# Two-layer hybrid decoder trunk on one core: the down product called block by block on a new pace, and sums formed beforehand given to other blocks

## The chip, the cores and the metric

The kernel runs on one core of a Trainium2 chip. The metric is device time in microseconds (us) of that core, from the start of the execution to its end; smaller is better. A profiled execution is one such run with the hardware profiler on; its span runs from the program's first to its last instruction.

Engine names: PE is the matrix engine (PEld its weight loads), DVE the vector engine, ACT the scalar engine, POOL the GpSimd engine, SP the engine that here only issues DMAs. Each engine works through a list of its own in order, and waits on semaphores for what others make.

## The reference

Two layers; each is a gated mixer and a SwiGLU feed-forward block over 256 tokens of width 2048, in float32. Only the feed-forward half is touched by the change; the mixer half is cut here.

```python
def reference(x, ...):
    for l in range(DEPTH):                       # DEPTH = 2
        ...
        x = x + mixed @ w_out[l]
        h2 = rms_norm(x, norm2_g[l])             # (1, 256, 2048)
        x = x + (jax.nn.silu(h2 @ w_gate[l]) * (h2 @ w_up[l])) @ w_down[l]
    return x                                     # w_gate, w_up: (2048, 5632); w_down: (5632, 2048)
```

## The kernel before, in words

**Exact products from split operands.** Each weight tile of 128 x 1024 float32 (512 KB) is loaded into a `raw` buffer (7 of them, filled by SP in the order of line 89) and split in two by `split2`: ACT casts it to `wh` (line 100, 5 buffers), DVE subtracts to get the rest, `wl` (line 101, 4 buffers). `mm3` then makes each product with three matmuls of 128 x 512 (lines 130, 131, 132). A tile of the plain product (`unit`) feeds 12 matmuls, a tile of the feed-forward product (`s_unit`) feeds 6, so one costs PE twice what the other does, and ACT and DVE the same.

**Gate and up together by a seven-product scheme.** The 5632 hidden columns are cut into NFF = 11 blocks of 512 (numbered 0 to 10). For each, `seven` forms gate and up at once with a Strassen-like scheme: 28 tiles instead of 32. In the first half of a block there are four pieces i = 0 to 3 of five tiles each; some of the tiles are sums of weights: `s1` (line 639), `t2` (line 640) and `b12` (line 644), three adds of 128 x 1024 on DVE for each piece. After `t2` has been used, another weight is added onto it by an accumulating DMA that POOL issues (line 647), and it is kept in one of four buffers. In the second half the block takes eight more tiles, four fresh loads `b21` and the four kept ones. Then come the small steps that end the block: four sums on PSUM banks, silu and multiply (lines 657 to 670), and the transposes `act_T` (PE line 194, ACT line 582, DVE line 583) that make the two `aT` pairs that the down product reads. A block yields 30 times, once for each tile and twice more; `k` counts these steps.

**Sums formed beforehand.** For six pairs (block, piece), listed in `PRE`, `presum` forms the three sums early in the layer, during the mixer, and writes them to DRAM (`sums`). Such a piece loads `s1`, `t2` and `b12` and DVE makes no adds for it. In the kernel before, these are pieces 2 and 3 of block 0 and all four of block 1. Where such a piece has an even i, the last weight isn't added onto `t2` by DMA: DVE adds it (line 679) from `b21` after that tile has been split.

**The down product beside it.** `down(blocks)` multiplies a group of finished blocks by `w_down`: for each of four column blocks n it takes two PSUM banks (`dacc`), copies the residual `xres` into them (ACT, line 702, one copy for each of two token tiles), runs two `unit`s for each block, and copies the banks back to `xres` (ACT, line 721). The same two banks serve every n, so the next n starts when the copies out and in are done. Call this a change of bank: four ACT copies. `std_stream` picks the blocks: before, it takes a group when at least `CHUNK[0]` = 2 blocks are finished and not yet taken (or all that are left), at most `CHUNK[1]` = 3. The main loop at the end of a layer (lines 752 to 762) walks through the steps of `seven` and, after each step, asks for down units until their number has caught up with a straight line in k. Before, that line starts at k = 60 and rises by 76 units in 270 steps; when no group is ready, the loop goes on with `seven` and catches up later. The last 12 units (`TAIL`) follow after the last block. The mixer's tail has taken the first 8 steps of `seven` already (`LEAD`).

The framework below then orders each engine's list by its own priorities, so lists differ a little from the order of the code.

Of the kernel before, what the change touches and what calls it, by code (L numbers as in the profile page):

```python
# [16 lines left out]
ALU = mybir.AluOpType  # L17
# [22 lines left out]
NI = 3584 // NB  # L40
NFF = DFF // NB
ND = D // NB
PRE = ((0, 2), (0, 3), (1, 0), (1, 1), (1, 2), (1, 3))
PRE_AT = ((20, 29, 38, 48, 57, 66), (4, 16, 28, 40, 54, 66))
LEAD = 8
STEPS = 30
CHUNK = (2, 3)
ACT_TILES = 8
TAIL = 12
WARM = 12  # L50
# [14 lines left out]
def trunk(ctx, tc, x, xt, w_in, w_out, w_gate, w_up, w_down, sgu_w, sgu_g, consts,  # L65
          band, out):
    nc = tc.nc
# [17 lines left out]
    def raw_load(src, parts=1):  # L85
        raw = wp.tile([P, 2, NB], F32, tag="raw", name="raw", bufs=7)
        n = 2 // parts
        for i in range(parts):
            last_load[0] = nc.sync.dma_start(
                raw[:, i * n : (i + 1) * n, :], src[:, i * n : (i + 1) * n, :]  # L90
            )
        return raw

    def split2(raw):
        wh = wp.tile([P, 2, NB], F32R, tag="wh", name="wh", bufs=5)
        wl = wp.tile([P, 2, NB], F32R, tag="wl", name="wl", bufs=4)
        step = 2 if clock[0] > 1 else 1
        for j in range(0, 2, step):
            src = raw[:, j : j + step, :]
            nc.scalar.copy(wh[:, j : j + step, :], src)  # L100
            nc.vector.tensor_tensor(  # L101
                wl[:, j : j + step, :], src, f(wh[:, j : j + step, :]), ALU.subtract
            )
        return wh, wl
# [5 lines left out]
    def later(delay, fn):  # L110
        pending.append((clock[0] + delay, next(serial), fn))
# [17 lines left out]
    def mm3(acc, ah, al, wh, wl, first, last, again=False):  # L129
        nc.tensor.matmul(acc, ah, wh, start=first, stop=False, skip_group_check=again)  # L130
        nc.tensor.matmul(acc, ah, wl, start=False, stop=False, skip_group_check=again)  # L131
        nc.tensor.matmul(acc, al, wh, start=False, stop=last, skip_group_check=again)  # L132
# [113 lines left out]
    for lay in range(L):  # L246
# [241 lines left out]
        sums = {}  # L488

        def presum(b, i, early, lay=lay, sums=sums):  # L490
            keep = dp.tile([3, P, 2, NB], F32, tag=f"sum{lay}_{b}_{i}", name="sums")
            t = []
            for w, q in ((w_gate, 0), (w_up, 0), (w_up, 1)):
                if early:
                    x = tp.tile([P, 2, NB], F32, tag="aT", name="pre")
                else:
                    x = ap.tile([P, 2, NB], F32, tag="spt", name="pre", bufs=4)
                with tc.issue_after(last_load[0].ins):
                    nc.sync.dma_start(x, w[lay, b, i, q])
                t.append(x)  # L500

            def add(k):
                nc.vector.tensor_tensor(t[k], t[k], t[(k + 1) % 3], ALU.add)
                nc.gpsimd.dma_start(keep[k], t[k])

            for k in range(3):
                later(2 + k, lambda k=k: add(k))
            sums[b, i] = keep

        for at, (b, i) in zip(PRE_AT[lay], PRE):  # L510
            later(at, lambda at=at, b=b, i=i: presum(b, i, at < 48))
# [90 lines left out]
        def seven(b, lay=lay, pairs2=pairs2, ext2=ext2, act_later=act_later, sums=sums, norm2=norm2):  # L602
            bank = [pa.tile([P, NB], F32, tag="acc", name=f"m{i}") for i in range(5)]

            def s_unit(raw, m, i, op, first, last, bank=bank):
                wh, wl = split2(raw)
                for j in range(2):
                    ah, al = (op(2 * i + j, h) for h in range(2))
                    mm3(
                        bank[m], ah, al, wh[:, j, :], wl[:, j, :], first and j == 0,  # L610
                        last and j == 1, m in (0, 2),
                    )
                tick(0.5)

            def a_op(k, t):
                return lambda p, h: pairs2[p][:, h, k, t * P : (t + 1) * P]

            def e_op(n):
                return lambda p, h: ext2[p][:, h, n, :]

            kept = []
            for i in range(4):
                pre = sums.get((b, i))
                b11 = raw_load(w_gate[lay, b, i, 0])
                t2 = ap.tile([P, 2, NB], F32, tag="spt", name="t2", bufs=4)
                if pre is not None:
                    s1 = raw_load(pre[0])
                    nc.sync.dma_start(t2, pre[2])
                    b22 = raw_load(w_up[lay, b, i, 1])
                    b12 = raw_load(pre[1])  # L630
                else:
                    s1 = b11
                    b12 = raw_load(w_up[lay, b, i, 0])
                    b22 = raw_load(w_up[lay, b, i, 1])
                first, last = i == 0, i == 3
                s_unit(b11, 0, i, a_op(0, 0), first, last)
                yield
                if pre is None:
                    nc.vector.tensor_tensor(s1, b11, b12, ALU.add)  # L639
                    nc.vector.tensor_tensor(t2, s1, b22, ALU.add)  # L640
                s_unit(s1, 1, i, e_op(1), first, last)
                yield
                if pre is None:
                    nc.vector.tensor_tensor(b12, b12, b22, ALU.add)  # L644
                s_unit(t2, 3, i, e_op(2), first, last)
                if pre is None or i % 2:
                    nc.gpsimd.dma_start(t2, w_gate[lay, b, i, 1], accum_op=ALU.add)  # L647
                yield
                s_unit(b22, 4, i, e_op(3), first, last)
                yield  # L650
                s_unit(b12, 2, i, e_op(0), first, last)
                yield
                kept.append(t2)
            m0, c12, c21, c22 = (
                zp.tile([P, NB], F32, tag="z", name=v) for v in ("m0", "c12", "c21", "c22")
            )
            nc.scalar.copy(m0, bank[0])
            nc.vector.tensor_tensor(m0, bank[3], m0, ALU.add)
            yield

            def add(out, x, y):
                nc.vector.tensor_tensor(out, x, y, ALU.add)

            def gated(t, psum, sg, c):
                nc.scalar.activation(sg, psum, AF.Silu, scale=norm2["r"][t])
                nc.vector.scalar_tensor_tensor(sg, c, norm2["n"][t], sg, ALU.mult, ALU.mult)

            steps = {
                0: lambda: add(c21, bank[2], m0),
                1: lambda: (nc.scalar.copy(bank[2], c21), add(c12, bank[1], m0)),  # L670
                2: lambda: (add(c22, bank[1], c21), add(c12, bank[4], c12)),
                5: lambda: gated(0, bank[0], m0, c12),
            }
            for i in range(8):
                if i < 4:
                    b21 = raw_load(w_gate[lay, b, i, 1])
                    s_unit(b21, 0, i, a_op(1, 0), False, i == 3)
                    if (b, i) in sums and i % 2 == 0:
                        nc.vector.tensor_tensor(kept[i], kept[i], b21, ALU.add)
                else:  # L680
                    s_unit(kept[i - 4], 2, i - 4, a_op(1, 1), False, i == 7)
                yield
                steps.get(i, lambda: None)()
            later(1, lambda: gated(1, bank[2], c21, c22))
            act_later(b, [m0, c21])
            yield
# [7 lines left out]
        left = [NFF]  # L694
# [32 lines left out]
        def std_stream(down=down, pairs_f=pairs_f, left=left):  # L727
            downed = set()
            while left[0]:
                full = [b for b in sorted(pairs_f) if len(pairs_f[b]) == 2 and b not in downed]  # L730
                if len(full) >= CHUNK[0] or left[0] == len(full):
                    blocks = full[: CHUNK[1]]
                    downed.update(blocks)
                    yield from down(blocks)
                else:
                    yield False
# [3 lines left out]
        k = 0  # L740
# [9 lines left out]
        norm2["n"] = [nr[:, t : t + 1] for t in range(NTOK)]  # L750

        other = std_stream()
        done = 0
        for _ in steps:
            k += 1
            ahead = (k - CHUNK[0] * STEPS) * (8 * NFF - TAIL)
            while done * (NFF - CHUNK[0]) * STEPS < ahead and next(other, False):
                done += 1
        seven_done[0] = True
        for went in other:  # L760
# [92 lines left out]
```

## Time and profile before

| what | value |
|---|---|
| three timed runs | 1984.83, 1986.64, 1988.50 us (median 1986.64) |
| profiled execution, own time | 1985.98 us |
| its span | 1984.3 us |
| DVE busy, whole span | 1722.3 us (87%) |
| ACT busy, whole span | 1327.5 us (67%) |
| blocks 1 to 10 of layer 0 (first to last m0 add, line 658) | 319.3 to 937.5 us |
| the same in layer 1 | 1307.2 to 1925.2 us |
| bytes read from HBM | 455.17 MB, 240 GB/s over the span with the writes |

How to read it: the feed-forward stretch of a layer runs from about 260 us to 985 us of the span, and again from about 1250 us to the end. The add that forms m0 at the end of a block's first 20 tiles (line 658) stands once in each block, so its eleven starts in a layer cut the stretch into ten equal pieces of work. A row of the windows view gives, for one stretch of time, the busy time of PE, PEld, DVE, ACT and POOL with their instruction counts, the granted PE clock, the busy share of the DMA engines and GB/s.

### The profile page before, as it was taken

How to read it: one execution, taken by the hardware profiler on the slowest of the kernel's cores; microseconds unless marked ns; L12 is line 12 of the kernel's file. 1: busy time of each engine (PE TensorE's matmuls, PEld its weight loads, DVE VectorE, ACT ScalarE, POOL GpSimd, SP SyncE). 2: the span in 40 equal slices, each digit the busy share in tenths (PEclk: the TensorE clock that was granted, in tenths of full speed). 3: DMA queues.
4: the chain of work that ended last, by engine and by line, in shares of the span. 5: the costliest groups of instructions: out<-in, count | busy, mean ns of one | idle time of the engine just before them, and what ended most of it. 6: DMA issues, size and time to landing. Idle time of an engine off the chain costs nothing.

```text
span 1984.3 us, 25315 instructions
## 1 busy us (share of the span) xinstructions
PE 1937.9 (98%) x8788; PEld 1566.9 (79%) x8788; DVE 1722.3 (87%) x1816; ACT 1327.5 (67%) x1759; POOL 144.4 (7%) x162
## 2 busy tenths in 40 slices
PE   9999999999999999999999999999999999999999
PEld 7788887788787887878887888877887878878787
DVE  6767789999999999998766767899999999999994
ACT  7576568666666766766856755586766767757675
POOL 1211000000000000000012110000000000000000
PEclk9999999999999999999999999999999999999999
DMA  9858678778676876778787576787777677867783
GB/s 375 311 193 291 232 226 282 235 244 274 201 233 224 255 226 220 226 215 255 270 273 259 188 248 217 236 282 234 236 255 218 229 232 244 257 201 224 225 254 133
DMA packets 133072, 477.81 MB, mean 241 GB/s; under 512 B 14800, under 2 KB 15440, under 8 KB 132944
## 3 DMA queue, kind: packets, MB, share of 16 engines
q1 hardware_dynamic: 113904, 406.98, 56.7%
q0 software_dynamic: 19040, 69.21, 16.5%
q8 instruction: 69, 1.13, 0.2%
q14 instruction: 59, 0.48, 0.1%
HBM read 455.17 MB, written 20.97 MB: 240 GB/s over the span
## 4 chain that ended last, share of the span: by engine, by line
PE 82%; DVE 8%; issue 5%; ACT 3%; DMA 2%; POOL 1%; SPq 0%; DVEq 0%; ACTq 0%; POOLq 0%
PE m L131 12%; PE m L130 12%; PE m L132 12%; PE dacc L130 7%; PE dacc L131 7%; PE dacc L132 7%; PE acc L131 7%; PE acc L132 7%; PE acc L130 7%; DVE wl L101 4%; ACT wh L100 2%; DMA raw<-in_w_down_dram 1%; DVE raw L644 1%; PE ps_v L367 1%; PE ps_f L194 1%
## 5 line engine op out<-in xcount | busy, mean ns | idle before, releaser
L100 ACT CAST wh<-raw 128x1024 fp32r<-128x1024 f32 (+1 forms) x794 | 812.8, 1049 | 432.9 <-DVE raw L639 147.4
L101 DVE TENSOR_TENSOR wl<-raw,wh 128x1024 fp32r<-128x1024 f32 (+1 forms) x794 | 945.4, 1217 | 130.1 <-PE acc L131 53.3
L130 PE MATMUL m<-wh,ext 128*128 128x512 f32 x704 | 279.7, 399 | 15.9 <-ACT wh L100 15.7
L130 PE MATMUL dacc<-wh,aT 128*128 128x512 f32 x736 | 287.5, 394 | 2.1 <-ACT dacc L702 1.7
L132 PE MATMUL dacc<-wh,aT 128*128 128x512 f32 x736 | 286.8, 390 | 0.0
L131 PE MATMUL dacc<-wl,aT 128*128 128x512 f32 x736 | 286.6, 389 | 0.0
L131 PE MATMUL m<-wl,ext 128*128 128x512 f32 x704 | 279.4, 397 | 5.7 <-DVE wl L101 5.7
L132 PE MATMUL m<-wh,ext 128*128 128x512 f32 x704 | 275.3, 392 | 0.0
L131 PE MATMUL m<-wl,hT 128*128 128x512 f32 x528 | 208.1, 394 | 7.6 <-DVE wl L101 7.4
L101 DVE TENSOR_TENSOR wl<-t,wh 128x1024 fp32r<-128x1024 f32 x176 | 211.5, 1218 | 3.1 <-ACT wh L100 1.9
L100 ACT CAST wh<-t 128x1024 fp32r<-128x1024 f32 x176 | 183.3, 1050 | 37.2 <-DVE t L640 16.4
L132 PE MATMUL m<-wh,hT 128*128 128x512 f32 x528 | 206.8, 392 | 0.1
L130 PE MATMUL m<-wh,hT 128*128 128x512 f32 x528 | 205.3, 393 | 1.4 <-ACT m L670 0.8
L130 PE MATMUL acc<-wh,hT 128*128 128x512 f32 x448 | 179.4, 403 | 0.4 <-ACT wh L100 0.4
L131 PE MATMUL acc<-wl,hT 128*128 128x512 f32 x448 | 176.0, 393 | 1.6 <-DVE wl L101 1.5
L132 PE MATMUL acc<-wh,hT 128*128 128x512 f32 x448 | 175.8, 393 | 0.0
L130 PEld LDWEIGHTS m<-wh,ext 128*128 128x128 f32 x704 | 133.1, 189 | 49.8 <-ACT wh L100 23.4
L647 POOL DMA_DIRECT2D t<-in_w_gate_dram x82 | 70.2, 856 | 1351.0 <-DVE wl L101 1220.8
L130 PEld LDWEIGHTS dacc<-wh,aT 128*128 128x128 f32 x736 | 137.8, 188 | 36.6 <-ACT dacc L702 4.4
L131 PEld LDWEIGHTS m<-wl,ext 128*128 128x128 f32 x704 | 133.0, 189 | 40.4 <-DVE wl L101 13.9
L132 PEld LDWEIGHTS dacc<-wh,aT 128*128 128x128 f32 x736 | 138.1, 188 | 29.1
L131 PEld LDWEIGHTS dacc<-wl,aT 128*128 128x128 f32 x736 | 138.2, 188 | 28.5 <-DVE wl L101 0.3
(132 smaller groups left out, 2450.2 us busy)
## 6 DMA issues: line engine op xcount, KB each, us to landing
raw<-in_w_gate_dram SPq DMA_DIRECT2D x176, 512.0 KB, 5.9
raw<-in_w_down_dram SPq DMA_DIRECT2D x176, 512.0 KB, 4.8
raw<-in_w_up_dram SPq DMA_DIRECT2D x164, 512.0 KB, 5.6
raw<-in_w_in_dram SPq DMA_DIRECT2D x108, 512.0 KB, 5.1
t<-in_w_gate_dram POOLq DMA_DIRECT2D x82, 512.0 KB, 6.0
raw<-in_w_out_dram SPq DMA_DIRECT2D x64, 512.0 KB, 4.5
sums<-pre POOLq DMA_DIRECT2D x36, 512.0 KB, 5.4
pre<-in_w_up_dram SPq DMA_DIRECT2D x24, 512.0 KB, 6.3
```

The source lines that it names most:

```text
L100: nc.scalar.copy(wh[:, j : j + step, :], src)
L101: nc.vector.tensor_tensor(wl[:, j : j + step, :], src, f(wh[:, j : j + step, :]), ALU.subtract)
L130: nc.tensor.matmul(acc, ah, wh, start=first, stop=False, skip_group_check=again)
L131: nc.tensor.matmul(acc, ah, wl, start=False, stop=False, skip_group_check=again)
L132: nc.tensor.matmul(acc, al, wh, start=False, stop=last, skip_group_check=again)
L194: nc.tensor.transpose(ps[:, j, t * P : (t + 1) * P], blocks[t][:, j * P : (j + 1) * P], ident)
L367: nc.tensor.matmul(pv[:, r, i], pt[:, (r * n + i) * (t + 1) + b, :], zkv[b][:, cols], start=b == 0, stop=b == t,)
L644: nc.vector.tensor_tensor(b12, b12, b22, ALU.add)
L647: nc.gpsimd.dma_start(t2, w_gate[lay, b, i, 1], accum_op=ALU.add)
```

## The change

Three edits, all in the feed-forward half.

1. **PRE**: pieces 1, 2 and 3 of block 1 lose their sums formed beforehand, and piece 0 of blocks 3, 5 and 7 get them. The number stays six a layer, and `presum` runs at the same places.
2. **The last weight on t2** is always added by the accumulating DMA; the DVE add of line 679 is gone.
3. **The down product's groups and pace**: a group is taken as soon as one block is finished (at most `MOST` = 3), and the straight line starts at k = `START` = 36 and rises by 76 units in 294 steps.

```diff
-PRE = ((0, 2), (0, 3), (1, 0), (1, 1), (1, 2), (1, 3))
+PRE = ((0, 2), (0, 3), (1, 0), (3, 0), (5, 0), (7, 0))
-CHUNK = (2, 3)
+START = 36
+MOST = 3
...
-                if pre is None or i % 2:
-                    nc.gpsimd.dma_start(t2, w_gate[lay, b, i, 1], accum_op=ALU.add)
+                nc.gpsimd.dma_start(t2, w_gate[lay, b, i, 1], accum_op=ALU.add)
...
-                    b21 = raw_load(w_gate[lay, b, i, 1])
-                    s_unit(b21, 0, i, a_op(1, 0), False, i == 3)
-                    if (b, i) in sums and i % 2 == 0:
-                        nc.vector.tensor_tensor(kept[i], kept[i], b21, ALU.add)
+                    s_unit(raw_load(w_gate[lay, b, i, 1]), 0, i, a_op(1, 0), False, i == 3)
...
-                if len(full) >= CHUNK[0] or left[0] == len(full):
-                    blocks = full[: CHUNK[1]]
+                if full:
+                    blocks = full[:MOST]
...
-            ahead = (k - CHUNK[0] * STEPS) * (8 * NFF - TAIL)
-            while done * (NFF - CHUNK[0]) * STEPS < ahead and next(other, False):
+            while done * (NFF * STEPS - START) < (k - START) * (8 * NFF - TAIL) and next(other, False):
```

**Where the loads of w_down stand on SP.** The next rows are SP's list at the start of block 6 of layer 0 in the kernel before; `raw<-in_w_down` is a tile of the down product, `raw<-in_w_gate` and `raw<-in_w_up` are tiles of `seven`, and a number behind x counts equal rows in a run.

```order
L89 DMA raw<-in_w_up_dram 128x1024 x2
L89 DMA raw<-in_w_down_dram 128x1024 x2
L89 DMA raw<-in_w_gate_dram 128x1024 x5
L89 DMA raw<-in_w_up_dram 128x1024 x2
L89 DMA raw<-in_w_gate_dram 128x1024
L89 DMA raw<-in_w_up_dram 128x1024 x2
L89 DMA raw<-in_w_down_dram 128x1024 x5
L89 DMA raw<-in_w_gate_dram 128x1024
```

The same place in SP's list of the changed kernel (line 90 is line 89 of before):

```order
L90 DMA raw<-in_w_up_dram 128x1024 x2
L90 DMA raw<-in_w_down_dram 128x1024
L90 DMA raw<-in_w_gate_dram 128x1024
L90 DMA raw<-in_w_down_dram 128x1024
L90 DMA raw<-in_w_gate_dram 128x1024 x3
L90 DMA raw<-in_w_down_dram 128x1024 x2
L90 DMA raw<-in_w_gate_dram 128x1024
L90 DMA raw<-in_w_up_dram 128x1024 x2
L90 DMA raw<-in_w_down_dram 128x1024
```

Before, ten tiles of `seven` stand between two tiles of the down product, and then five of those in a row; now there are one to three between single ones or pairs.

**How far apart the changes of bank stand on ACT.** ACT's list of before, from the end of one change of bank to the start of the next, around the end of block 2 (`dacc` are the two banks, `CAST wh` the casts that every tile needs):

```order
L702 COPY dacc_3917<-xres 128x512
L100 CAST wh<-raw 128x1024
L665 ACTIVATE c_3779<-m_3394,ir_2740 128x512
L100 CAST wh<-raw 128x1024 x2
L100 CAST wh<-t_3945 128x1024
L100 CAST wh<-raw 128x1024 x4
L582 CAST aT<-ps_f 128x512 x2
L100 CAST wh<-raw 128x1024
L100 CAST wh<-t_4042 128x1024
L100 CAST wh<-raw 128x1024 x5
L721 COPY xres<-dacc_3916 128x512
```

And in the changed kernel, in block 3 (lines 699, 718 and 101 are 702, 721 and 100 of before):

```order
L699 COPY dacc_4221<-xres 128x512
L699 COPY dacc_4222<-xres 128x512
L101 CAST wh<-raw 128x1024 x6
L101 CAST wh<-t_4265 128x1024
L101 CAST wh<-raw 128x1024 x3
L718 COPY xres<-dacc_4221 128x512
L718 COPY xres<-dacc_4222 128x512
L699 COPY dacc_4361<-xres 128x512
L699 COPY dacc_4362<-xres 128x512
```

Between two changes of bank stood 15 casts, now 10.

**What DVE does in piece 0 of block 3.** Before, from the last kept tile of block 2 on (lines 639, 640 and 644 are the three adds of a piece):

```order
L101 TENSOR_TENSOR wl<-t_3700,wh 128x1024
L101 TENSOR_TENSOR wl<-raw,wh 128x1024 x2
L639 TENSOR_TENSOR raw<-raw 128x1024
L640 TENSOR_TENSOR t_3945<-raw 128x1024
L666 SCALAR_TENSOR_TENSOR c_3779<-c_3780,nr,c_3779 128x512
L101 TENSOR_TENSOR wl<-raw,wh 128x1024 x2
L644 TENSOR_TENSOR raw<-raw 128x1024
L101 TENSOR_TENSOR wl<-t_3945,wh 128x1024
```

The same place in the changed kernel (line 102 is line 101 of before):

```order
L102 TENSOR_TENSOR wl<-t_3832,wh 128x1024
L102 TENSOR_TENSOR wl<-raw,wh 128x1024 x3
L102 TENSOR_TENSOR wl<-t_4059,wh 128x1024
L666 SCALAR_TENSOR_TENSOR c_3911<-c_3912,nr,c_3911 128x512
L102 TENSOR_TENSOR wl<-raw,wh 128x1024 x3
L584 TENSOR_TENSOR aT<-ps_f,aT 128x512
```

The three adds are gone from this piece, and only splits are left.

## The prediction

> **What bounds the kernel now.** I read the page's first part, then windows of 50 us, then windows cut at the blocks, then the waits of DVE and ACT within them.
>
> ```profile
> span 1984.3 us, 25315 instructions
> PE 1937.9 (98%) x8788; PEld 1566.9 (79%) x8788; DVE 1722.3 (87%) x1816; ACT 1327.5 (67%) x1759; POOL 144.4 (7%) x162
> 800.00:850.00 50.00, 50.00 (x226) 41.28 (x225) 47.83 (x47) 35.15 (x43) 2.56 (x3) 1.00 0.70 218
> 850.00:900.00 50.00, 47.01 (x196) 36.11 (x194) 47.15 (x46) 34.01 (x39) 2.55 (x3) 0.97 0.71 231
> ```
>
> PE's 98% looks like a kernel with nothing left, but the two windows below it differ: 226 matmuls in one, 196 in the other, with PE busy 50.00 and 47.01. The fuller window gives PE's pace, 50 / 226 = 0.221 us a matmul; at that pace the second had 30 x 0.221 = 6.6 us free. Counts of instructions, not busy time, show PE's slack here. The Trainium skill ("Perfetto Trace Analysis", section Identifying the Most-Contended Engine) says so as a rule and asks for the busy share of weight loads instead. By it the 79% of PEld would leave 21%, some 417 us, open; but the full window loads weights for only 41.28 of 50 us, 83%, so the trace leaves about 4 points (roughly 80 us), and I go by the trace.
>
> Now the same by blocks, layer 0, from one m0 add to the next (columns: length, then PE, PEld, DVE, ACT, POOL busy, clock, DMA share, GB/s):
>
> ```profile
> L658 DVE TENSOR_TENSOR m<-m,m x11: 680/682/691, 319.3 to 937.5; 128x512 f32<-128x512 f32 x11
> 319.30:359.70 40.40, 39.34 (x174) 31.29 (x173) 38.95 (x39) 33.98 (x37) 1.69 (x2) 1.00 0.93 318
> 359.70:420.70 61.00, 56.93 (x242) 45.20 (x242) 58.56 (x57) 38.21 (x43) 3.40 (x4) 0.97 0.70 217
> 420.70:484.30 63.60, 63.05 (x281) 51.41 (x280) 62.06 (x60) 44.40 (x52) 3.41 (x4) 1.00 0.75 240
> 484.30:548.40 64.10, 61.62 (x272) 49.66 (x271) 60.83 (x58) 43.40 (x50) 3.42 (x4) 1.00 0.72 230
> 548.40:611.80 63.40, 63.40 (x283) 51.73 (x282) 61.21 (x58) 43.55 (x52) 3.42 (x4) 1.00 0.74 239
> 611.80:677.30 65.50, 63.27 (x279) 51.09 (x278) 62.12 (x60) 44.34 (x52) 3.40 (x4) 1.00 0.73 227
> 677.30:739.50 62.20, 62.20 (x278) 51.09 (x278) 60.89 (x58) 43.16 (x52) 3.41 (x4) 1.00 0.75 242
> 739.50:805.50 66.00, 63.68 (x275) 51.19 (x274) 61.13 (x59) 44.21 (x53) 3.44 (x4) 0.97 0.74 225
> 805.50:868.00 62.50, 62.13 (x276) 50.59 (x275) 60.92 (x57) 43.24 (x51) 3.40 (x4) 1.00 0.73 234
> 868.00:937.50 69.50, 66.82 (x284) 52.91 (x284) 63.29 (x61) 45.95 (x54) 3.40 (x4) 0.98 0.72 222
> ```
>
> DVE is busy about 61 us in each full block whatever the block's length: the ten rows add up to 590.0 us of 618.2. PE needs 0.221 x 276 = 61.0 us of its own. **Two engines are level, DVE a little ahead**, with buffers of four `wl` tiles between them, so whatever makes DVE idle lengthens the block. Good blocks take 62.2 to 63.6 us; every second one takes 64.1, 65.5, 66.0 and 69.5. What makes these longer:
>
> ```profile
> DVE aT L583 <- ACT aT L582: 9.8, 6, 2.4
> DVE wl L101 <- ACT wh L100: 4.0, 9, 0.7
> DVE wl L101 <- PE dacc L131: 3.5, 3, 2.5
> DVE wl L101 <- ACT dacc L702: 0.9, 1, 0.9
> ACT wh L100 <- DMA raw<-in_w_down_dram: 16.6, 7, 4.2
> ```
>
> (waits in 319.3 to 937.5: total us, times, longest). One such place, in DVE's and ACT's rows of the timeline:
>
> ```profile
> 508.43 4.62 DVE L101 TENSOR_TENSOR wl<-raw,wh 128x1024 fp32r<-128x1024 f32 x4
> 515.36 0.69 DVE L583 TENSOR_TENSOR aT<-ps_f,aT 128x512 fp32r<-128x512 f32 x1 [2.32 <-ACT aT L582]
> 513.80 1.05 ACT L100 CAST wh<-raw 128x1024 fp32r<-128x1024 f32 x1 [3.69 <-DMA raw<-in_w_down_dram]
> 507.94 5.76 DMA raw<-in_w_down_dram
> ```
>
> The last row is the chain of waits itself. A pair of blocks is used up before the next pair is finished, so `seven` runs alone (DVE sets the pace), and then the down product catches up in a run of loads. The first of them lands 5.76 us after its issue, ACT stands 3.69 us at its cast, and behind it in ACT's list stands the cast of `aT` for which DVE idles 2.32 us. In the run itself PE is the slow one, and DVE waits for it (`PE dacc`). Layer 0 has four such starts.
>
> **The change, part by part**, for one layer and for the stretch from block 0's m0 add to block 10's:
>
> ```profile
> L679 DVE TENSOR_TENSOR t<-t,raw x6: 1212/1217/1226, 316.4 to 1352.1; 128x1024 f32<-128x1024 f32 x6
> L640 DVE TENSOR_TENSOR t<-raw 128x1024 f32<-128x1024 f32 x36 | 44.0, 1222 | 0.9
> L101 DVE TENSOR_TENSOR wl<-raw,wh 128x1024 fp32r<-128x1024 f32 x274 | 324.1, 1218 | 11.9 <-PE dacc L131 3.5 <-ACT wh L100 3.0 <-issue 2.8
> L702 ACT COPY dacc<-xres 128x512 f32<-128x512 f32 x36 | 20.9, 593 | 0.4
> L721 ACT COPY xres<-dacc 128x512 f32<-128x512 f32 x36 | 20.6, 583 | 11.9 <-PE dacc L132 11.9
> SPq L628 <- DVE wl L101: 2.1, 3, 0.7
> t<-in_w_gate_dram POOLq DMA_DIRECT2D x82, 512.0 KB, 6.0
> ```
>
> *Adds removed.* Three of line 679 a layer at 1.22 us on an engine that is the bound: **-3.7 us** (bounds -3.7 and 0, if PE then ends last). In their place POOL issues three more accumulating DMAs, each landed in about 6.0 us and first read nine tiles later or more; behind them in POOL's list stand only others of their kind. Nothing. (One of the three adds stands just ahead of the stretch, at 316.4.)
>
> *Runs gone.* In the new order one down unit follows every two to four tiles of `seven`; the line asks for 8 units in 8 x 294 / 76 = 31 steps, and a block is finished every 30, so no group runs out. The four starts' waits go: 9.8 less two short ones of 0.2 is 9.4 us, and 3.5 us on PE's banks: **-13 us**. Bounds: 0, if the late load only moves to another cast, and -16, with the 2.8 us that DVE's splits waited for no cause that the profile names. What is late next is PE itself.
>
> *Changes of bank.* Before, the groups are (0,1), (2,3), (4,5), (6,7), (8,9) and (10): 6 x 4 = 24 changes. Now 11 x 4 = 44, so 20 more, each with 2 x 0.583 + 2 x 0.593 = 2.35 us on ACT: 47 us a layer. ACT was busy 43 to 46 us of a full block and has room for 4.7 more, but its list is in order: behind the copy that waits for PE's last matmul stand the casts that DVE and then PE need. The 36 copies out in this stretch are 18 changes; DVE's waits for `wh` and for the copy in (4.0 + 0.9 us) make 0.27 us each. 20 x 0.27 = **+5.4 us**. Bounds: 0 (the waits are elsewhere) and 20 x 0.9 = +18, at the longest single wait. I stay at the mean, since the banks now change ten casts apart, never within a run. For PE, ten casts leave several tiles of work between a bank's last matmul and its next first.
>
> *Sums given to other blocks.* Six pieces as before, three adds each, so DVE's sum is unchanged. In block 1, which ran without down units, they served fully: 40.40 us long, DVE 38.95, PE 39.34. A summed piece beside 1.33 down units (five of 30 steps, eight units) costs DVE 6.33 x 1.22 = 7.7 us and PE (30 + 16) x 0.221 = 10.2 us, so DVE would idle 2.5 us unless it works ahead; four `wl` buffers hold 4.9 us of splits. For blocks 3, 5 and 7 that is 0 to +7.4 us; two thirds carried over leave **+2.5 us**. Block 1 now gets down units early, which is what keeps it level: about 4 of them. The load of `t2` stands in SP's list and has waited at most 0.7 us for its buffer, with the loads behind it; DMA was 0.93 busy in the summed block 1 without delaying PE there, so I cost this at nothing.
>
> Sum for a layer: -3.7 - 13 + 5.4 + 2.5 = -8.8 us. Block 0 before its m0 add, the mixer and the tail (both kernels end with 4 units of earlier blocks and 8 of block 10) stay. Two layers: **-17.6 us**. Against the profiled execution's own time, 1985.98 (span 1984.3 and 1.7 around it), that is 1968.4; the median of the runs lies 0.7 higher, so I say 1969.
>
> *The clock.* The granted clock fell in three blocks of layer 0, and in none of their twins in layer 1:
>
> ```profile
> 1348.00:1407.50 59.50, 55.21 (x241) 43.79 (x241) 58.63 (x57) 38.05 (x43) 3.43 (x4) 1.00 0.69 217
> 1726.50:1793.00 66.50, 62.43 (x275) 49.88 (x274) 61.12 (x58) 44.10 (x52) 3.41 (x4) 1.00 0.73 222
> 1855.60:1925.20 69.60, 65.68 (x284) 51.69 (x283) 63.25 (x61) 45.81 (x54) 3.42 (x4) 1.00 0.70 221
> ```
>
> Lengths with a dip 61.0, 66.0 and 69.5; without, 59.5, 66.5 and 69.6. The dips cost +1.5 - 0.5 - 0.1 = 0.9 us in all, so even if they go I count nothing. The Trainium skill ("TensorE: Matmul & The Clock Gate", Part 1) puts a closed gate at half speed for a window of about 3.4 us; by it three windows would cost an estimated 5 us, and the sum would be near -23. The rows of layer 1 speak against that.
>
> **The rivals.**
>
> *All waits go.* Each block becomes like the best (62.2), the changes of bank hide behind PE, and the summed pieces carry over in full: -3.7 - 16 = -19.7 us a layer, 1986 - 39 = 1947. For it: the good blocks idle DVE by only 1.3 us. Against: two engines this level rarely stay so.
>
> *Slower by ACT's list.* The mechanism is the change of bank. The terms without it sum to -14.2 us, so 20 changes break even at 0.71 us each; DVE's single waits of this kind reached 0.7 and 0.9 us. At 0.95 us each a layer gains 20 x 0.95 - 14.2 = +4.8 us, 1996. For it: ACT's copies out waited 11.9 us in 36, for PE. Against: the mean of 0.27, and that the longest of those waits are in runs, where the copy follows its matmuls at once.
>
> *Nothing gained.* PE takes over: each catch-up went at PE's pace, and a block's 0.221 x 276 = 61.0 us stays. If the adds and half of the starts' waits are gained and the banks and summed pieces take 10 us, a layer changes by -3.7 - 6.5 + 10 = -0.2 us: 1986.
>
> *The change doesn't do what it says*, a block not being finished in time: the list orders show even spacing, so I give this nothing of its own.
>
> **How the numbers follow.** The forecast, 1955 to 1981: 0.58. All waits go, 1943 to 1955: 0.18. Nothing gained, 1981 to 1991: 0.16. Slower, above 1991: 0.08. The range, 1948 to 1988, leaves out 0.06 below, 0.05 of the case of nothing gained and the 0.08 of slower, 0.19 in all. About 0.2%, 4 us, is what a measurement of this kernel can tell from no change; so faster (below 1982.7) has 0.58 + 0.18 + 0.03 = 0.79, within 0.2% 0.13, slower 0.08.
>
> **What would show it.** Right: no block of 2 to 10 over 64 us; DVE's waits for `aT` under 3 us a layer and ACT's waits for `in_w_down` loads under 5; 176 copies into the banks in the whole run (before 96); 88 accumulating DMAs. Wrong: DVE idle more than 28 us a layer, with waits for `wh` or the bank copies above 10 us (the ACT rival), or blocks 3, 5 and 7 no shorter than blocks 2, 4 and 6 (summed pieces wasted).

## The result

| kernel | median | lowest to highest | ratio to before, 95% interval |
|---|---|---|---|
| before | 1987.01 us (4 runs) | 1984.83 to 1988.50 | 1 |
| changed | 1956.76 us (4 runs) | 1956.19 to 1958.38 | 0.985 (0.9833 to 0.9867) |

The changed kernel is 30 us faster, 1.5%. Its profiled execution took 1958.38 us with a span of 1956.2. The page's first part, of the changed kernel:

```profile
span 1956.2 us, 25423 instructions
PE 1932.7 (99%) x8788; PEld 1565.3 (80%) x8788; DVE 1714.9 (88%) x1810; ACT 1402.3 (72%) x1919; POOL 148.9 (8%) x168
```

PE has the same 8788 matmuls. DVE has six instructions less, ACT 160 more and is 75 us busier. Next the blocks of layer 0 in the changed kernel, from one m0 add to the next (columns as before: length, then busy time and count of PE, PEld, DVE, ACT, POOL, then clock, DMA share, GB/s):

```profile
319.20:371.60 52.40, 50.79 (x216) 38.97 (x215) 51.55 (x51) 38.05 (x45) 3.39 (x4) 1.00 0.76 236
371.60:434.00 62.40, 61.74 (x273) 49.90 (x272) 60.88 (x59) 47.76 (x59) 3.41 (x4) 1.00 0.74 236
434.00:494.70 60.70, 60.70 (x272) 49.78 (x271) 57.69 (x56) 47.54 (x59) 3.41 (x4) 1.00 0.81 260
494.70:555.60 60.90, 60.61 (x267) 48.62 (x266) 59.77 (x58) 45.79 (x58) 3.44 (x4) 1.00 0.72 239
555.60:616.10 60.50, 59.94 (x268) 49.14 (x267) 57.59 (x56) 46.77 (x58) 3.41 (x4) 1.00 0.80 254
616.10:678.40 62.30, 61.92 (x276) 50.40 (x275) 61.10 (x59) 46.36 (x59) 3.41 (x4) 1.00 0.74 238
678.40:737.70 59.30, 59.30 (x266) 48.81 (x265) 56.52 (x54) 45.66 (x58) 3.43 (x4) 1.00 0.80 262
737.70:800.20 62.50, 61.90 (x272) 49.63 (x272) 61.11 (x59) 46.63 (x59) 3.43 (x4) 1.00 0.72 235
800.20:862.30 62.10, 61.34 (x271) 49.56 (x270) 60.98 (x59) 46.61 (x56) 3.41 (x4) 1.00 0.73 232
862.30:924.60 62.30, 61.86 (x273) 49.86 (x273) 60.81 (x58) 47.59 (x59) 3.41 (x4) 1.00 0.74 236
```

The long blocks of 64 to 69.5 us are gone, and no block is over 62.5. The ten pieces hold the same tiles of `seven`, but not equal work, as the matmul counts show: block 1 now has 216 instead of 174, because down units run beside it, and block 10 has 273 instead of 284. So the whole stretch is the fair comparison; 76 loads of `w_down` stand in it in both kernels. DVE's busy time is nearly what it was, 588.0 us in ten blocks (before 590.0); its idle time fell from 28.2 to 17.4. The stretch takes 605.4 us instead of 618.2, 12.8 less, and in layer 1 (1294.3 to 1899.2) 604.9 instead of 618.0, 13.1 less. With 2.1 us at the end of layer 1 that is the whole difference of the spans. DVE's waits in the stretch (total us, times, longest), changed kernel:

```profile
DVE wl L102 <- ACT wh L101: 10.9, 25, 1.0
DVE wl L102 <- issue: 1.2, 2, 0.8
DVE wl L102 <- PE dacc L132: 1.0, 1, 1.0
DVE wl L102 <- PE m L132: 0.4, 1, 0.4
DVE c L662 <- PE m L133: 0.2, 1, 0.2
DVE aT L584 <- ACT aT L583: 0.5, 1, 0.5
```

The waits for `aT` and for PE's banks went from 9.8 and 3.5 us to 0.5 and 1.0. The waits for ACT's casts grew from 4.0 (and 0.9 for a copy into the banks) to 10.9. Both signs were forecast; the balance came out larger.

Of the signs that the prediction named for being right, all came: the longest of blocks 2 to 10 takes 62.5 us, DVE waits 0.5 us for `aT`, and ACT's waits for loads of `w_down` (the same stretch), the accumulating DMAs and the copies into the banks (152 and 24, together 176) read:

```profile
ACT wh L101 <- DMA raw<-in_w_down_dram: 0.3, 1, 0.3
t<-in_w_gate_dram POOLq DMA_DIRECT2D x88, 512.0 KB, 5.8
L699 ACT COPY dacc<-xres x152: 581/592/616, 307.2 to 1902.2; 128x512 f32<-128x512 f32 x152
L699 ACT COPY acc<-xres x24: 581/591/605, 926.1 to 1941.3; 128x512 f32<-128x512 f32 x24
```

One half of a sign of being wrong came too: the waits for `wh` are above 10 us. The other half, DVE idle more than 28 us, did not.

### The profile page after: what moved, and what is told of

Same layout as the page of the kernel before. It is cut to its first block, busy times and chain, and to the rows that moved or that the text cites. A ratio compares the mean times of both kernels' runs of the same rounds, so it can differ in the third digit from the quotient of the medians.

```text
span 1956.2 us, 25423 instructions
## 1 busy us (share of the span) xinstructions
PE 1932.7 (99%) x8788; PEld 1565.3 (80%) x8788; DVE 1714.9 (88%) x1810; ACT 1402.3 (72%) x1919; POOL 148.9 (8%) x168
## 4 chain that ended last, share of the span: by engine, by line
PE 76%; DVE 12%; issue 7%; ACT 4%; DMA 1%; POOL 1%; SPq 0%; DVEq 0%; ACTq 0%; POOLq 0%
PE m L132 11%; PE m L131 11%; PE m L133 10%; DVE wl L102 7%; PE acc L132 7%; PE dacc L131 7%; PE acc L133 7%; PE acc L131 7%; PE dacc L132 7%; PE dacc L133 7%; ACT wh L101 2%; DVE raw L640 2%; DVE t L641 1%; PE ps_f L195 1%; PE ps_v L368 1%
## 5 line engine op out<-in xcount | busy, mean ns | idle before, releaser
L647 POOL DMA_DIRECT2D t<-in_w_gate_dram x88 | 75.4, 857 | 1340.5 <-DVE wl L102 1165.3
```

## The experiments

Each ratio is against runs of the kernel before on the same chip; all carry a 95% interval. Theory W says that the catch-up runs cost and that the even spacing removes them; the rivals are named in the expectations.

| label | what differs | median, us | ratio (interval) |
|---|---|---|---|
| pace_alone | before, with new groups and line | 1960.63 | 0.9874 (0.9859 to 0.9889) |
| spread_alone | before, with the new PRE | 2012.12 | 1.0133 (1.0118 to 1.0149) |
| adds_alone | before, without the DVE adds | 1989.00 | 1.002 (1.0011 to 1.003) |
| old_sums | changed, with the old PRE | 1957.76 | 0.9864 (0.9848 to 0.988) |
| single_old_line | before, with single blocks | 1959.15 | 0.9869 (0.9855 to 0.9882) |
| runs_of_four | changed, down units in runs | 2014.39 | 1.0144 (1.0128 to 1.0159) |
| double_banks | changed, twice the changes of bank | 1986.65 | 1.0007 (0.9998 to 1.0016) |
| no_sums | changed, no sums beforehand | 1982.77 | 0.9988 (0.9979 to 0.9997) |
| before_raw8 | before, eight raw buffers | 1980.07 | 0.9974 (0.9964 to 0.9984) |
| sums_early | changed, sums in blocks 0 and 1 only, other pieces | 1955.47 | 0.9849 (0.9836 to 0.9863) |
| sums_early_raw8 | the same with eight raw buffers | 1957.98 | 0.9865 (0.985 to 0.9881) |
| pairs_slow_line | before, with a slower line | 1965.71 | 0.9898 (0.9883 to 0.9914) |

**The three parts, one at a time.** `pace_alone` is the changed kernel with these lines put back:

```diff
-PRE = ((0, 2), (0, 3), (1, 0), (3, 0), (5, 0), (7, 0))
+PRE = ((0, 2), (0, 3), (1, 0), (1, 1), (1, 2), (1, 3))
...
+                if pre is None or i % 2:
+                    nc.gpsimd.dma_start(t2, w_gate[lay, b, i, 1], accum_op=ALU.add)
...
+                    if (b, i) in sums and i % 2 == 0:
+                        nc.vector.tensor_tensor(kept[i], kept[i], b21, ALU.add)
```

> The new groups and pace alone; the sums stay with block 1 and the DVE add of line 679 stays. Theory W (the even pace removes the waits at the starts of the catch-up runs, some 16 us a layer, and pays about 6 us a layer in changes of bank; the sums only keep blocks level): blocks 2 to 10 take about 62.4 us each as the changed kernel's blocks without sums do, block 1 about 50, so 612 us a layer for the stretch against 605 in the changed kernel: about 1969 us. Rival S (the spread sums carry the gain, because they relieve DVE where down units run beside the block, and the pace alone only trades waits for changes of bank): 1980 us or more.

Measured 1960.63, 24.4 us under the kernel before on its chip. Rival S falls; W's number was 8 us too high. Its interval and that of the changed kernel overlap only at their ends.

`spread_alone` is the kernel before with only this:

```diff
-PRE = ((0, 2), (0, 3), (1, 0), (1, 1), (1, 2), (1, 3))
+PRE = ((0, 2), (0, 3), (1, 0), (3, 0), (5, 0), (7, 0))
```

> The sums spread to blocks 1, 3, 5 and 7, with the old groups of two blocks, the old pace and the DVE add. Theory W: the four catch-up starts a layer stay, and block 1, without down units beside it, loses three of its summed pieces where DVE alone sets the pace: 1987 us, between 1982 and 1994. Rival S: 1972 us or less.

Measured 2012.12, 27 us slower than before. W's number was too low as well, though its reason shows. Block 1 of layer 0 in `spread_alone`:

```profile
320.50:369.50 49.00, 42.28 (x171) 31.43 (x170) 48.33 (x48) 32.94 (x37) 2.53 (x3) 0.97 0.67 209
```

Without down units beside it and with three summed pieces fewer, the block takes 49.0 us instead of 40.4; DVE is busy all but 0.7 us, and PE has only 171 matmuls to do. That is 8.6 of the 14.0 us by which the stretch of layer 0 is longer. The blocks that got the sums return nothing in all: blocks 3, 5 and 7 took 62.9, 63.8 and 67.2 us (before 63.6, 63.4 and 62.2). In block 7 another effect of this edit shows. The DVE add of line 679 stays here for summed pieces with an even i, and the new list has five such pieces a layer instead of three, so there are 10 of these adds in the run instead of 6. One of them makes DVE wait in block 7 for its load:

```profile
DVE t L679 <- DMA raw<-in_w_gate_dram: 2.8, 1, 2.8
```

The changed kernel has none of these adds, so the 27 us are not the price of moving the sums alone.

`adds_alone` is the kernel before with only this:

```diff
-                if pre is None or i % 2:
-                    nc.gpsimd.dma_start(t2, w_gate[lay, b, i, 1], accum_op=ALU.add)
+                nc.gpsimd.dma_start(t2, w_gate[lay, b, i, 1], accum_op=ALU.add)
...
-                    if (b, i) in sums and i % 2 == 0:
-                        nc.vector.tensor_tensor(kept[i], kept[i], b21, ALU.add)
```

> Only the three DVE adds a layer of line 679 are replaced by accumulating DMAs. Theory W: 3 x 1.22 us a layer at most where DVE is the bound, so 1980 to 1985 us. Rival P (PE ends last in those blocks, so the adds were hidden): 1987 us.

Measured 1989.00, 0.2% slower than before, which neither W nor P gave. ACT's waits in block 1 of layer 0, `adds_alone`, and then the block's window:

```profile
ACT wh L100 <- DMA raw<-sums: 3.5, 3, 2.1
ACT wh L100 <- PE m L132: 2.8, 5, 1.5
ACT wh L100 <- DMA raw<-in_w_up_dram: 1.8, 1, 1.8
ACT wh L100 <- DMA raw<-in_w_gate_dram: 1.4, 1, 1.4
```

```profile
319.40:363.00 43.60, 42.23 (x185) 33.32 (x184) 39.27 (x40) 32.70 (x36) 3.38 (x4) 1.00 0.96 310
```

ACT waits 6.7 us for loads there; in the kernel before it waited 0.6 in that block, with the DMA engines 0.93 busy. With two more accumulating transfers the DMA share there rises to 0.96, and the block takes 43.6 us instead of 40.4. That these transfers hold up the loads is the likely reading; no run changes them alone. Block 2, where another of the adds is gone, takes 58.3 us instead of 61.0, so the stretch of layer 0 is even 0.5 us shorter (617.7); in layer 1 it is 1.4 us longer (619.4). The rest of the 2.5 us by which the span grew lies outside the stretches, so block 1 explains why nothing is gained, not the whole 0.2%.

`old_sums` is the changed kernel with the old PRE line (the first pair of lines of `pace_alone`).

> The changed kernel with the sums put back to blocks 0 and 1, so new pace and no DVE add. Theory W: 3 to 7 us below the pace alone, about 1964 us. Rival S: 1976 us or more, since the spread is missing.

Measured 1957.76, against 1956.76 of the changed kernel: their intervals overlap, so with the new pace the place of the sums makes no difference that shows. Rival S falls. The blocks say why: 3, 5 and 7 take 61.3, 61.5 and 60.1 us with the old PRE and 60.7, 60.5 and 59.3 with the new, 2.4 us in all, and block 1 takes 49.5 and 52.4, 2.9 us the other way. Over the whole stretch the new PRE is 1.0 us shorter in layer 0 and 0.4 in layer 1. Block 1 of `old_sums`:

```profile
318.70:368.20 49.50, 47.75 (x209) 37.88 (x208) 43.11 (x42) 38.52 (x44) 3.39 (x4) 1.00 0.97 323
```

Its four summed pieces leave DVE idle for 6.4 us, since the new pace puts down units beside this block; that is why taking three of them away costs so little.

**Runs, pairs and the line.** `single_old_line` is `pace_alone` with the old line, so the kernel before with only the size of the groups changed:

```diff
-START = 36
+START = 60
```

> The kernel before with one thing changed: single finished blocks instead of pairs, with the old sums, the old DVE add and the old line (from k = 60, 76 units in 270 steps). By that line a single block is always there in time. Theory W (the catch-up runs cost what they cost because a pair isn't ready): the runs go and the changes of bank come, so most of the pace's 25 us is there already: 1962 to 1970 us. Rival E (the gain is the early start, down units beside block 1, and the slower line that evens PE and DVE): 1978 us or more.

Measured 1959.15: all of the pace's gain, so rival E falls. Four of its windows in layer 0 (blocks 4, 5, 9 and 10):

```profile
484.40:547.60 63.20, 63.20 (x282) 51.56 (x281) 62.01 (x59) 48.69 (x61) 3.44 (x4) 1.00 0.74 236
547.60:610.90 63.30, 62.60 (x276) 50.45 (x275) 62.17 (x59) 48.06 (x61) 3.42 (x4) 1.00 0.72 238
798.40:862.30 63.90, 63.53 (x281) 51.48 (x280) 63.08 (x59) 48.98 (x61) 3.41 (x4) 1.00 0.74 233
862.30:925.40 63.10, 63.03 (x283) 51.83 (x282) 62.19 (x59) 49.23 (x60) 3.41 (x4) 1.00 0.74 242
```

The slots that took up to 69.5 us before take 63 to 64, with DVE idle about 1 us and up to 283 matmuls done. In the whole stretch DVE idles 15.6 us instead of 28.2, with the same 76 loads of `w_down` in it. The earlier start and slower line of the change add nothing that shows.

`pairs_slow_line` goes the other way: the kernel before with pairs kept, and a line that pairs can feed:

```diff
-TAIL = 12
+TAIL = 18
...
-            ahead = (k - CHUNK[0] * STEPS) * (8 * NFF - TAIL)
-            while done * (NFF - CHUNK[0]) * STEPS < ahead and next(other, False):
+            ahead = (k - 70) * (8 * NFF - TAIL)
+            while done * (NFF * STEPS - 70) < ahead and next(other, False):
```

> The kernel before (groups of two, old sums, old DVE add, 24 changes of bank a layer) with a line that pairs can feed: from k = 70, 70 units in 260 steps, so 18 units follow after the last block instead of 12, and no run of down units is left in the list. Theory W (the runs cost, whatever the group's size): 1959 us as with single blocks, less some 40 changes of bank at 0.2 us, and more for 6 units a layer that move from beside the blocks into the tail, where PE takes 2.7 us each and DVE stands by, less 1.2 us of DVE work each in the blocks: 1959 - 8 + 18 = 1969 us, between 1960 and 1975. Rival P (pairs cost by themselves, in the order of transposes and banks): 1980 us or more.

Measured 1965.71, where W put it. Blocks 4, 6, 8 and 10 of layer 0, the long ones before:

```profile
477.00:539.00 62.00, 61.95 (x276) 50.57 (x275) 60.99 (x59) 43.43 (x51) 3.42 (x4) 1.00 0.73 243
600.80:662.70 61.90, 61.64 (x274) 50.12 (x273) 60.80 (x58) 43.59 (x51) 3.41 (x4) 1.00 0.76 238
725.50:787.00 61.50, 61.50 (x275) 50.39 (x274) 60.67 (x58) 43.73 (x51) 3.44 (x4) 1.00 0.73 239
848.80:910.90 62.10, 61.72 (x273) 50.02 (x272) 60.67 (x59) 43.31 (x51) 3.41 (x4) 1.00 0.73 238
```

DVE's idle time in the stretch falls from 28.2 to 9.5 us, with pairs and without one more change of bank. So the runs cost and not the pairs. This run alone leaves a rival, that six down units fewer beside the blocks relieve PE; `single_old_line`, with all 76, leaves none. (This line pays elsewhere, since more down units follow the blocks: the way from block 10 of layer 0 to block 0 of layer 1 takes 387 us instead of 370, and that from block 10 of layer 1 to the end 74 instead of 59.)

`runs_of_four` puts runs into the changed kernel:

```diff
-            while done * (NFF * STEPS - START) < (k - START) * (8 * NFF - TAIL) and next(other, False):
+            while k % 15 == 0 and done * (NFF * STEPS - START) < (k - START) * (8 * NFF - TAIL) and next(other, False):
```

> The changed kernel, but down units are asked for only at every 15th step, so they come in runs of about four; their number, the sums and the changes of bank are the same. Theory W: each run costs about what a start of before cost, 16 us a layer over 4 starts = 4 us, and there are some 19 a layer: 1957 + 150 = 2107 us, and not below 2040. Rival L (only a late load at the first start after a long pause costs, and a run that comes regularly is loaded in time): 1965 to 1990 us.

Measured 2014.39, 58 us more than the changed kernel: 1.5 us for each of some 38 runs, between the theories. Waits of DVE, then of PE, in its stretch of layer 0:

```profile
DVE wl L102 <- PE dacc L132: 16.4, 25, 1.4
DVE wl L102 <- ACT wh L101: 8.4, 17, 0.9
DVE wl L102 <- ACT dacc L699: 7.1, 5, 1.5
```

```profile
PE m L131 <- ACT wh L101: 19.1, 36, 1.0
PE m L132 <- DVE wl L102: 1.5, 2, 0.8
```

Both engines wait in turn: DVE for PE inside the runs (16.4 us), PE for the casts between them (19.1 us; 2.2 in the changed kernel). No late load of `w_down` shows in ACT's waits here. A run costs by itself, but only a third of what a start of the kernel before did.

**The late load.** `before_raw8` gives the kernel before one more `raw` buffer (`bufs=7` to `bufs=8` in `raw_load`).

> The kernel before with eight raw buffers in place of seven, nothing else: SP may issue each load one tile earlier. Theory L (a start of before costs more than a regular run, some 4.4 against 1.5 us, because the first load of w_down lands late and holds ACT's list): with the load a tile earlier about half of that wait goes, 8 starts x 1.5 to 2 us: 1970 to 1976 us. Rival R (the run itself costs, PE and DVE out of step after a long pause, and the late load is only what the wait is put down to): 1983 us or more.

Measured 1980.07, 5 us faster. ACT's wait for loads of `w_down` in the stretch fell from 16.6 to 5.4 us, and DVE's wait for `aT` from 9.8 to 6.7; its waits for casts and for PE's banks hardly moved:

```profile
DVE aT L583 <- ACT aT L582: 6.7, 5, 2.2
DVE wl L101 <- ACT wh L100: 4.3, 10, 0.7
DVE wl L101 <- PE dacc L131: 4.3, 3, 2.5
```

Neither theory's number was met. The stretches are 4.3 and 4.6 us shorter, nearly all of it in blocks 1, 2 and 4 (block 4 of layer 0 takes 62.0 us instead of 64.1); blocks 6, 8 and 10 of layer 0 stay at 65.5, 65.9 and 69.2. With two thirds of the late loads' wait gone, most of the starts' price remains, so the late load is the smaller part of it.

**The price of a change of bank.** `double_banks` is the changed kernel with `down` opening and closing the banks for each unit:

```diff
-                acc = new_acc() if seven_done[0] else new_acc(pd, "dacc")
-                for t in range(NTOK):
-                    nc.scalar.copy(acc[t], xres[:, t, n * NB : (n + 1) * NB])
                 for k, b in enumerate(blocks):
                     for c in range(2):
+                        acc = new_acc() if seven_done[0] else new_acc(pd, "dacc")
+                        for t in range(NTOK):
+                            nc.scalar.copy(acc[t], xres[:, t, n * NB : (n + 1) * NB])
                         pair = pairs_f[b][c]
-                        unit(
-                            w_down[lay, b, n, c], [(pair, 0), (pair, 1)], acc,
-                            False, k == len(blocks) - 1 and c == 1, True,
-                        )
+                        unit(w_down[lay, b, n, c], [(pair, 0), (pair, 1)], acc, False, True, True)
...
+                        if not (k == len(blocks) - 1 and c == 1):
+                            for t in range(NTOK):
+                                nc.scalar.copy(xres[:, t, n * NB : (n + 1) * NB], acc[t])
```

> The changed kernel with a change of bank after each down unit instead of after two: 44 more a layer, 88 in all, each with four ACT copies. Theory W (0.27 us each, what DVE waits for ACT): 88 x 0.27 = +24, about 1981 us. Rival A (ACT's list is the next bound, over 0.7 us each): 2018 us or more. Rival N (the changes are hidden, the wait only moves): 1960 us or less.

Measured 1986.65, 30 us more than the changed kernel or 0.34 us for each of 88. In the stretch of layer 0 (first and last m0 add):

```profile
L658 DVE TENSOR_TENSOR m<-m,m x11: 680/684/692, 322.1 to 934.4; 128x512 f32<-128x512 f32 x11
```

That is 612.3 us against 605.4, so 6.9 us for about 37 more changes, 0.19 us each. The rest lies where no block runs beside: from block 10 of layer 0 to block 0 of layer 1 (374.6 against 369.7 us) and from block 10 of layer 1 to the end (64.8 against 57.0), 12.7 us for the 14 or so changes that fall there, 0.9 us each; the stretch of layer 1 has 7.5 us more, and 2.9 us come ahead of block 0's m0 add in layer 0, which nothing here explains. Rivals A and N both fall; W's sum was 24 us.

**What the sums are worth.** `no_sums` is the changed kernel with `PRE = ()`.

> The changed kernel without any sums formed beforehand: six pieces a layer make their three adds on DVE. Theory W: the three pieces in blocks 3, 5 and 7 are worth some 0.8 us each beside down units (60.7 against 61.3 us and the like), those of blocks 0 and 1, where DVE alone sets the pace, 3.7 us each: 2 x (2.4 + 11) = +27, about 1984 us, less what DVE gains in the mixer without the 18 adds a layer, which PE bounds: nothing. Rival S2 (with the even pace all sums are hidden): 1960 us or less.

Measured 1982.77, near W's 1984. Block 0's m0 add comes at 324.9 us instead of 319.2, for two pieces 2.9 us each, and block 1 takes 57.7 us instead of 52.4, 5.3 us for its one piece, more than the 3.7 us of its three adds; why isn't known. Rival S2 falls.

**A better version.** `sums_early` is the changed kernel with `PRE = ((0, 1), (0, 2), (0, 3), (1, 0), (1, 1), (1, 2))`, `sums_early_raw8` the same with eight raw buffers.

> The changed kernel with the six pieces at (0,1), (0,2), (0,3), (1,0), (1,1), (1,2), where few or no down units run beside them. Theory W (a summed piece is worth about 2.9 us where DVE alone sets the pace and 0.8 us beside down units): 2.9 - 0.5 = 2.4 us a layer less than the changed kernel with the old sums (1958): about 1953 us. Rival S2 (sums are all hidden once the pace is even, and piece 1 of block 0 falls into the mixer's tail): 1957 us or more.

> The same with eight raw buffers. Theory L: the even pace has no late loads left to speak of (waits of ACT for loads below 4 us a layer), so 0 to 4 us less. Rival: a deeper ring helps everywhere, 8 us or more less.

Measured 1955.47 and 1957.98. The first has the lowest median of all kernels here, but its interval overlaps that of the changed kernel, so it is not shown to be better; it lies between what W and S2 gave. The deeper ring gives nothing: the fastest of its four runs, 1956.82 us, is slower than the slowest of `sums_early`, 1955.85.

## Why the prediction was right, and where it was off

The measured 1956.76 us lies in the stated range, and faster was right. The forecast gain was 17.6 us and the measured one 30 (28.1 by the spans), so the terms have to be gone through.

- **Bound.** DVE and PE level: right. `runs_of_four` shows both waiting in turn, and block 1 of `spread_alone` shows DVE alone setting the pace where no down units run. That DVE is a little ahead beside down units isn't shown. That DVE's idle time lengthens the blocks is: in layer 0 the stretch is 12.8 us shorter, of which 10.8 are idle time of DVE and 2.0 busy time.
- **Runs gone, -13 us a layer: the term that was mis-sized.** The two kinds of waits that it counted went nearly as forecast, `aT` and `PE dacc` together from 13.3 to 1.5 us in layer 0. But DVE had more waits in that stretch of the kernel before:

```profile
DVE wl L101 <- issue: 2.8, 4, 1.2
DVE c L666 <- ACT c L665: 2.0, 3, 1.7
DVE wl L101 <- PE m L131: 0.9, 1, 0.9
DVE m L658 <- PE m L132: 0.7, 1, 0.7
DVE c L662 <- PE m L132: 0.2, 1, 0.2
```

  These 6.6 us became 1.8, so 16.6 us of waits are gone and not 13; the forecast had the 2.8 us only in its bound of 16, and the rest nowhere. A second way agrees: `single_old_line` shortens the stretch by 12.5 us in layer 0 and 14.9 in layer 1 (605.7 and 603.1 us), mean 13.7, and pays 20 changes of bank, 3.8 us at the 0.19 each of `double_banks`, which makes 17.5. The step that failed is the choice of rows: I summed the waits that I had seen at the four starts, not all of DVE's idle time that an uneven order could cause. Whether each of the other waits came from a run isn't shown one by one. The lengths of neighbouring blocks would not have told more: the even ones of 64.1, 65.5, 66.0 and 69.5 us are 13.4 us over four times the mean of the odd ones.
- **The late load** as the start's mechanism: only in small part. One more buffer took two thirds of ACT's wait for it and gave 8.9 us in the two stretches, of some 33 to 35 (5 in the whole run). Why a start of before cost about three times a run of `runs_of_four` isn't settled: on SP's list both the pauses before it (7 to 13 tiles of `seven`, against 7 to 10) and the runs (4 to 7 units, against 3 or 4) were longer, which no run here separates.
- **Changes of bank, +5.4 us a layer:** about right. DVE's waits for casts and copies into the banks grew by 6.0 us in layer 0; `double_banks` gives 0.19 us each beside blocks, so 3.8. The rival that ends slower needed 0.71 us and falls.
- **Adds removed, -3.7 us: wrong.** Alone they gave +0.2%. Beside the new pace (`pace_alone` against `old_sums`) the times differ by 3 us or less, within the intervals: in the stretch of layer 0 DVE's busy time falls from 590.2 to 588.1 us, and its idle time rises from 15.9 to 18.4. I had priced the accumulating DMAs by their landing time in an ordinary stretch, not by the block where the DMA share is 0.93.
- **Sums given to other blocks, +2.5 us:** measured about nothing (1.0 and 0.4 us shorter over the stretches), by two errors that cancel, which is luck. I had two thirds of what DVE saves in blocks 3, 5 and 7 carried over; DVE's busy time fell there by 3.0 to 3.3 us each, and the blocks by only 0.6 to 1.0. And I had block 1 pay for its three pieces in full; it paid 2.9 us, since DVE had stood idle there beside the new down units. The sign that blocks 3, 5 and 7 are shorter than 2, 4 and 6 says little: in `old_sums`, without sums in them, 5 and 7 are shorter than 6 as well (61.5 and 60.1 against 62.5 us).
- **The clock, nothing:** right. The dips of layer 0 are gone in the blocks of the changed kernel, and the gain of the stretch is the same in layer 1, where there were none (13.1 against 12.8 us).
- **All waits go, 1947:** too far; 17.4 us of DVE's idle time stay in a layer.

In the sum for layer 0: -16.6 for the waits gone, +6.0 for the casts and copies and -2.0 of DVE's busy time make -12.6 of the measured -12.8 us. The forecast of -8.8 fell short mainly by the waits that it left out; that it overrated the adds and counted 2.5 us for the sums nearly cancels.

## What to carry to other kernels

Where two engines are about equally loaded and only a few tiles can wait between them, work of one kind should not come in runs (runs of four cost this kernel 58 us): space the heavier kind by a line that its supply can always feed, and check the line against the supply before making groups larger. To price a run where one engine sets the pace, take all of that engine's idle time in the stretch, every kind of wait and the unnamed ones too, and not only the waits seen at the runs: here 16.6 us went, against 13 counted. Give work away in advance only where one engine alone sets the pace: a piece's sums were worth 2.9 us in block 0 and 0.6 to 1.0 us beside down units.

## What the runs showed of the hardware that was not expected

- Taking three adds a layer off DVE gained nothing; the kernel was 0.2% slower (1.0011 to 1.003). In block 1, where DMA engines 0.93 busy got two more accumulating transfers, ACT's wait for loads grew from 0.6 to 6.7 us and the block by 3.2 us in layer 0 and 2.3 in layer 1.
- The same four ACT copies cost 0.19 us beside blocks and about 0.9 us behind the last block, where for the most part the down product runs alone (12.7 us for some 14 changes, in `double_banks`).
